# Broadcast weights loaded over all 128 partitions at once: a three-neighbour interpolation kernel

## The chip, the core and the metric

The kernel runs on one core of one Trainium2 chip. The metric is the device time of one execution in microseconds (us). The time before is the median of three runs; one more execution was profiled, and all stretches and waits below are from that one.

## What is computed

For each of 16 batches there are 1024 reference vectors of 64 numbers. Each of 4096 queries names three of them by index and has three weights; the weights are divided by their sum, and the output is the weighted sum of the three vectors.

```python
# features (16, 1024, 64) f32, indices (16, 4096, 3) in 0..1023, weights (16, 4096, 3) f32
weights_norm = weights / (weights.sum(axis=2, keepdims=True) + 1e-8)
for b in range(16):
    for i in range(4096):
        for k in range(3):
            result[b, i] += weights_norm[b, i, k] * features[b, indices[b, i, k]]
```

## The kernel before

The gather is done as a matrix product with one-hot columns. A batch's features lie as 128 rows of eight consecutive vectors; four products of 128 x 128 (two vectors of 64 each, hence the four "planes" j) cover the eight. An index thus splits into a row (7 bits), a plane (2 bits) and a last bit that says which of the two vectors in the 128 output rows is meant.

**Preparation** (`prep`, lines 73 to 135) works on 4096 queries per batch laid out as 128 partitions of 32, for four batches at a time (the first batch alone, then three). VectorE (DVE) turns indices into 16-bit codes, and the weights into two fp16 copies, `wh[0]` and `wh[1]`: a weight stands in the one that its index's last bit names, and the other holds zero there. `put` (line 105) writes codes and both copies to scratch in HBM, `code_d` as [batch, k, query] and `wt_d` as [copy, batch, k, query], in pieces of 32 numbers, 64 bytes.

**Groups.** The main loop runs over groups of 2048 queries, two for each batch; the first batch is cut as 512, 512, 1024, 2048 so that it starts sooner. `load_codes` (151) broadcasts a group's codes from scratch to all 128 partitions of the tile `bcc`. `load_weights` (158) fills the tile `bcw` with two transfers: copy 0 goes to partitions 0 to 63, copy 1 to 64 to 127. In both, a partition's row is three runs of 2048 numbers (4 KB), one for each k. Each tile has three buffers. `load_features` (167) brings a batch's features, `cast_features` (171) makes them fp16 on ScalarE (ACT), in the same order.

**Stages of a chunk of 512 queries.** `stage1` (176): ACT turns codes into bytes `y` with one bit for each plane, set in the partition that the index names. `stage2` (183): DVE takes one bit for each of the four planes, which gives `s`, read as fp8. `main` (192): 12 matmuls of 128 x 512 on TensorE (PE), three k by four planes, into the PSUM tile `acc` (two buffers). `weight` (204): the product with the chunk's part of `bcw` gives `x`; even chunks read PSUM on DVE directly, odd ones through a copy `xc` by ACT. `back` (218): 12 matmuls of 128 x 64 with the matrix `i2` (two identities of 64 over each other) add the two halves of the 128 rows and the three k, and turn the result to queries in rows; it runs two chunks later. Every second chunk ACT copies the result to `og`, and SyncE (SP) starts the output transfer.

**Order.** Every engine works its instructions in the order in which the program gives them (`InOrder`, line 50; so the profile shows line 55 for nearly all, and groups are told apart by tile names). A table `todo` holds a time in chunks for each step: for a group that begins at chunk a, the codes are loaded at a - 12, the weights at a - 7, stage 1 runs from a - 8 on, one piece a chunk, stage 2 from a - 3 on. All transfers are issued by SP, on one queue, and SP waits in order too: an output transfer that waits for its copy holds up the loads behind it.

Of the kernel before, what the change touches and what calls it, by code (L numbers as in the profile page):

```python
# [9 lines left out]
P = 128  # L10
# [3 lines left out]
def kernel(  # L14
# [11 lines left out]
    nc = tc.nc  # L26
    fp32 = mybir.dt.float32
    fp16 = mybir.dt.float16
    fp8 = mybir.dt.float8e4
    i16 = mybir.dt.int16  # L30
# [5 lines left out]
    B, R, D = features.shape  # L36
    _, Q, K = indices.shape
    T = Q // P
    J = 4
    CH = 512  # L40
    GM = 2048
# [16 lines left out]
    pe, ve, ac, sp = (InOrder(e) for e in (nc.tensor, nc.vector, nc.scalar, nc.sync))  # L58

    sb = ctx.enter_context(tc.tile_pool(name="sb", bufs=2))  # L60
    ps = ctx.enter_context(tc.tile_pool(name="ps", bufs=2, space=bass.MemoryType.PSUM))

    i2_np = np.concatenate([np.eye(D), np.eye(D)], 0).astype(np.float16)
    i2_d = nc.inline_tensor(i2_np, name="i2")
    i2 = sb.tile([P, D], fp16, bufs=1, name="i2_sb")
    bias_d = nc.inline_tensor(
        (-8.0 * ((np.arange(P, dtype=np.float32) + 64) % 128 - 64))[:, None].copy(), name="lane")
    bias = sb.tile([P, 1], fp32, bufs=1, name="lane_sb")

    code_d = nc.dram_tensor("code_d", [B, K, Q], i16, kind="Internal")  # L70
    wt_d = nc.dram_tensor("wt_d", [2, B, K, Q], fp16, kind="Internal")

    def prep(b0, n):

        bs = slice(b0, b0 + n)
        NK = n * K

        def tl(dt, w, name):
            return sb.tile([P, PB * w], dt, bufs=1, name=name)[:, 0:n * w]

        idx = tl(i64, T * K, "idx")
        wt = tl(fp32, T * K, "wt")
        wt4 = wt.rearrange("p (b t k) -> p b t k", b=n, k=K)
        idk = tl(i32, K * T, "idk")
        lane = tl(i32, K * T, "lane_i")
        ex = tl(i32, K * T, "ex")
        code = tl(u16, K * T, "code")
        hb = tl(i32, K * T, "hb")
        ws = tl(fp32, T, "ws")
        wi = tl(fp32, T, "wi")  # L90
        wn = tl(fp16, K * T, "wn")
        wh = [tl(fp16, K * T, "wh%d" % h) for h in range(2)]
        v = ve

        def loads():
            sp.dma_start(out=idx.rearrange("p (b t k) -> p b t k", b=n, k=K),
                              in_=indices[bs].rearrange("b (p t) k -> p b t k", t=T))
            sp.dma_start(out=wt4, in_=weights[bs].rearrange("b (p t) k -> p b t k", t=T))

        def weigh(k):  # L100
            v.tensor_tensor(
                out=wn.rearrange("p (b k t) -> p b k t", b=n, k=K)[:, :, k, :],
                in0=wt4[:, :, :, k], in1=wi.rearrange("p (b t) -> p b t", b=n), op=Alu.mult)

        def put(dst, src):
            sp.dma_start(out=dst.rearrange("b k (p t) -> p (b k) t", t=T),
                              in_=src.rearrange("p (x t) -> p x t", t=T))

        return [
            loads,  # L110
            lambda: v.tensor_copy(
                out=idk.rearrange("p (b k t) -> p b k t", b=n, k=K),
                in_=idx.bitcast(i32).rearrange("p (b t k w) -> p b k t w", b=n, k=K, w=2)[:, :, :, :, 0]),
            lambda: v.tensor_scalar(out=lane, in0=idk, scalar1=6, scalar2=127 << 9,
                                    op0=Alu.logical_shift_left, op1=Alu.bitwise_and),
            lambda: v.tensor_scalar(out=ex, in0=idk, scalar1=23, scalar2=3 << 24,
                                    op0=Alu.logical_shift_left, op1=Alu.bitwise_and),
            lambda: v.tensor_scalar(out=ex, in0=ex, scalar1=134 << 23, scalar2=None,
                                    op0=Alu.bitwise_xor),
            lambda: v.scalar_tensor_tensor(out=code, in0=ex.bitcast(fp32), scalar=0.5, in1=lane,  # L120
                                           op0=Alu.mult, op1=Alu.add),
            lambda: put(code_d.ap()[bs], code.bitcast(i16)),
            lambda: v.tensor_reduce(out=ws, in_=wt.rearrange("p (x k) -> p x k", k=K),
                                    axis=mybir.AxisListType.X, op=Alu.add),
            lambda: v.tensor_scalar(out=ws, in0=ws, scalar1=1e-8, scalar2=None, op0=Alu.add),
            lambda: v.reciprocal(out=wi, in_=ws),
            lambda: weigh(0),
            lambda: weigh(1),
            lambda: weigh(2),
            lambda: v.tensor_scalar(out=hb, in0=idk, scalar1=1, scalar2=None, op0=Alu.bitwise_and),  # L130
            lambda: v.tensor_tensor(out=wh[1], in0=wn, in1=hb, op=Alu.mult),
            lambda: v.tensor_tensor(out=wh[0], in0=wn, in1=wh[1], op=Alu.subtract),
            lambda: put(wt_d.ap()[0, bs], wh[0]),
            lambda: put(wt_d.ap()[1, bs], wh[1]),
        ]


    groups = []
    for b in range(B):
        q = 0  # L140
# [8 lines left out]
    bcc, bcw, fsts, f16s, ys, ss = {}, {}, {}, {}, {}, {}  # L149

    def load_codes(g):
        b, q, n, _ = groups[g]
        bcc[g] = sb.tile([P, K * GM], i16, bufs=3, name="bcc")[:, 0:K * n]
        sp.dma_start(
            out=bcc[g].rearrange("p (k q) -> p k q", k=K),
            in_=code_d.ap()[b, :, q:q + n].unsqueeze(0).to_broadcast([P, K, n]))

    def load_weights(g):
        b, q, n, _ = groups[g]
        bcw[g] = sb.tile([P, K * GM], fp16, bufs=3, name="bcw")[:, 0:K * n].rearrange(  # L160
            "p (k q) -> p k q", k=K)
        for h in range(2):
            sp.dma_start(
                out=bcw[g][h * D:(h + 1) * D],
                in_=wt_d.ap()[h, b, :, q:q + n].unsqueeze(0).to_broadcast([D, K, n]))

    def load_features(b):
        fst = fsts[b] = sb.tile([P, J * P], fp32, bufs=2, name="fst")
# [2 lines left out]
    def cast_features(b):  # L171
        fst = fsts[b]
        f16s[b] = sb.tile([P, J, P], fp16, bufs=2, name="f16")
        ac.mul(out=f16s[b].rearrange("p j m -> p (j m)"), in_=fst[:, :], mul=0.5)

    def stage1(g, c):
        if c == 0:
# [65 lines left out]
    for g, (b, q, n, a) in enumerate(groups):  # L243
        m = n // CH
        at(a - 12, 0, load_codes, g)
        at(a - 7, 0, load_weights, g)
        if q == 0:
            at(-11.5 if b == 0 else max(a - 14, -4), 0, load_features, b)
            at(-8.6 if b == 0 else a - 3, 1, cast_features, b)
        for c in range(m):  # L250
            at(a - 2 * m + c if m == 4 else -8.5 + g / 10, 1, stage1, g, c)
        for j in range(J):
            at(a - m + (j * m // J | 1 if m == 4 else 0), 0, stage2, g, j)
    NCH = B * Q // CH
    for b0 in range(PB, B, PB):
        for s, step in enumerate(prep(b0, PB)):
            at((b0 - 4) * (Q // CH) + (s and s + 3), 0, step)
    first, second = prep(0, 1), prep(1, PB - 1)
    at(-20, 0, first[0])
    at(-20, 0, second[0])  # L260
# [71 lines left out]
```

## Time and profile before

| | |
|---|---|
| median of three runs | 529.38 us (524.7 to 532.22) |
| profiled execution, its own time | 525.81 us |
| its span, first to last instruction | 523.7 us |
| mean granted TensorE clock | 0.954 |
| busy: PE, ACT, DVE | 413.8, 320.3, 305.0 us |
| moved by DMA | 125.66 MB, mean 240 GB/s |

In the slices, a span is cut into 40 equal parts, and a digit is the busy share of a part in tenths. A group's row has the engine, the operation, what it writes and reads with shapes and count, then busy time, mean nanoseconds of one, the idle time of the engine before them, and what ended most of that. In the waits: who waited for whom, microseconds in total, how many times, the longest. "x" before a count is the number of instructions. A DMA share of 1.00 means that all 16 DMA engines worked the whole stretch; values just over that come from packets that are counted where they begin.

### The profile page before, as it was taken

Reading aid. Unit: us, or ns where it says so; the run is one execution under the profiler, and the core shown is the slowest. Engines: PE = TensorE matmul, PEld = TensorE weight load, DVE = VectorE, ACT = ScalarE, POOL = GpSimd, SP = SyncE. Lnnn points to the kernel's source line nnn. Section 1 sums busy time; section 2 is a strip of 40 time slices with the busy share of each in tenths; the row PEclk is TensorE's granted clock in tenths of the full one; section 3 lists DMA queues with packets and bytes.
Section 4 is the critical chain, followed back from the end, with each engine's and each line's share of the span. In section 5 each row is a group of like instructions: output and inputs, shape, how many; then the busy total and the mean of one; then the engine's idle time right before and its main releaser. Section 6 shows DMA issues by size and latency. Waiting matters only on the chain.

```text
span 523.7 us, 7372 instructions
## 1 busy us (share of the span) xinstructions
PE 413.8 (79%) x3072; PEld 209.8 (40%) x3072; DVE 305.0 (58%) x335; ACT 320.3 (61%) x274; POOL 0.2 (0%) x4
## 2 busy tenths in 40 slices
PE   0442797968979788978798777987888897998895
PEld 0110353434544444444344333444434443454453
DVE  5142377755556496766466465676646664665672
ACT  1444737765656867756566765567767674667723
POOL 0000000000000000000000000000000000000000
PEclk9986899998998999999999989999989999798998
DMA  3899999899999999899999999889999999999711
GB/s 71 239 175 237 260 258 264 213 262 216 248 283 277 292 283 281 215 235 265 227 284 281 296 273 239 202 208 281 220 260 301 288 281 276 263 266 246 232 41 61
DMA packets 70704, 125.66 MB, mean 240 GB/s; under 512 B 24080, under 2 KB 44048, under 8 KB 70672
## 3 DMA queue, kind: packets, MB, share of 16 engines
q1 hardware_dynamic: 70672, 125.20, 93.4%
q8 instruction: 24, 0.39, 0.3%
q14 instruction: 8, 0.07, 0.0%
HBM read 107.23 MB, written 17.96 MB: 239 GB/s over the span
## 4 chain that ended last, share of the span: by engine, by line
DMA 61%; ACT 12%; PE 10%; SPq 6%; issue 6%; DVE 4%; ACTq 0%
DMA bcc<-code_d 55%; PE acc L55 10%; SPq L55 6%; ACT xc L55 6%; ACT y L55 4%; DMA out_dram<-og 4%; DVE x L55 2%; ACT og L55 2%; DMA fst<-in_features_dram 2%; DVE s L55 1%; ACT f L55 1%; PE pr L55 1%; DMA idx<-in_indices_dram 0%; DMA code_d<-code 0%; ACTq L55 0%
## 5 line engine op out<-in xcount | busy, mean ns | idle before, releaser
L55 PE MATMUL acc<-s,f 128*128 128x512 fp8e4 x1536 | 377.7, 394 | 104.5 <-ACT xc L55 68.2
L55 ACT ACTIVATE y<-bcc,lane_sb 128x1536 uint8<-128x1536 int16 x128 | 198.3, 1577 | 148.5 <-DMA bcc<-code_d 148.5
L55 PEld LDWEIGHTS <-f 128*128 128x128 f16 x1536 | 148.4, 101 | 278.9 <-issue 119.0
L55 DVE TENSOR_TENSOR x<-xc,bcw 128x1536 f16<-128x1536 f16 x64 | 61.3, 958 | 159.1 <-ACT xc L55 158.8
L55 DVE TENSOR_SCALAR s<-y 128x1536 int32<-128x1536 int32 (+2 forms) x136 | 117.1, 905 | 14.6 <-ACT y L55 14.5
L55 DVE TENSOR_TENSOR x<-acc,bcw 128x1536 f16<-128x1536 f32 x64 | 112.2, 1753 | 17.6 <-PE acc L55 14.7
L55 ACT CAST xc<-acc 128x1536 f16<-128x1536 f32 x64 | 91.4, 1428 | 30.8 <-PE acc L55 30.8
L55 PEld LDWEIGHTS <-x 128*128 128x128 f16 x1536 | 71.9, 117 | 31.2 <-DVE x L55 1.8
L55 PE MATMUL pr<-i_sb,x 128*128 128x64 f16 x1536 | 72.2, 198 | 1.7 <-DVE x L55 1.7
L55 ACT COPY og<-pr 128x512 f32<-128x512 f32 x64 | 37.8, 591 | 5.4 <-DMA out_dram<-og 3.9
L55 ACT ACTIVATE f<-fst 128x512 f16<-128x512 f32 x16 | 10.2, 640 | 12.8 <-DMA fst<-in_features_dram 12.8
L55 DVE COPY idk<-idx 128x384 int32<-128x384 int32 (+2 forms) x5 | 2.5, 499 | 21.4 <-DMA idx<-in_indices_dram 21.3
L55 DVE RECIPROCAL wi<-ws 128x128 f32<-128x128 f32 (+2 forms) x5 | 3.9, 789 | 0.1
L55 DVE TENSOR_TENSOR wn<-wt,wi 128x128 f16<-128x128 f32 (+2 forms) x15 | 3.9, 282 | 0.1
L55 ACT ACT_TABLE_LOAD x1 | 1.3, 1283 | 2.8 <-DMA lane_sb<-lane 2.8
L55 DVE SCALAR_TENSOR_TENSOR code<-ex,lane_i 128x384 uint16<-128x384 f32 (+2 forms) x5 | 2.4, 474 | 0.4 <-DMA code_d<-code 0.3
L55 DVE TENSOR_TENSOR wh<-wn,hb 128x384 f16<-128x384 f16 (+2 forms) x5 | 2.4, 475 | 0.1
L55 DVE TENSOR_REDUCE ws<-wt 128x128 f32<-128x384 f32 (+2 forms) x5 | 2.3, 466 | 0.0
L55 DVE TENSOR_SCALAR lane_i<-idk 128x384 int32<-128x384 int32 (+2 forms) x5 | 1.6, 317 | 0.1
L55 DVE TENSOR_SCALAR ex<-ex 128x384 int32<-128x384 int32 (+2 forms) x5 | 1.6, 316 | 0.1
L55 DVE TENSOR_TENSOR wh<-wn,wh 128x384 f16<-128x384 f16 (+2 forms) x5 | 1.6, 314 | 0.1
L55 DVE TENSOR_SCALAR ex<-idk 128x384 int32<-128x384 int32 (+2 forms) x5 | 1.6, 314 | 0.0
(8 smaller groups left out, 3.4 us busy)
## 6 DMA issues: line engine op xcount, KB each, us to landing
bcc<-code_d SPq DMA_DIRECT2D x31, 1536.0 KB, 18.9
bcw<-wt_d SPq DMA_DIRECT2D x62, 768.0 KB, 20.1
out_dram<-og SPq DMA_DIRECT2D x64, 256.0 KB, 14.7
fst<-in_features_dram SPq DMA_DIRECT2D x16, 256.0 KB, 16.1
idx<-in_indices_dram SPq DMA_DIRECT2D x3, 384.0 KB, 21.4
bcc<-code_d SPq DMA_DIRECT2D x2, 384.0 KB, 8.7
bcc<-code_d SPq DMA_DIRECT2D x1, 768.0 KB, 13.1
bcw<-wt_d SPq DMA_DIRECT2D x4, 192.0 KB, 10.0
```

Source lines behind the costliest of these rows:

```text
L55: return tc.keep_in_program_order(getattr(self.engine, op)(*a, **kw))
```

## The change

Three things change together.

1. **Weights.** The two copies go to neighbouring partitions: copy 0 to the even ones, copy 1 to the odd ones, in one transfer over all 128 partitions. Row m of `acc` must then belong to vector m % 2 and number m // 2, so `cast_features` interleaves the two vectors as it writes (a step of two in its output), and `i2` becomes an identity with each row twice. The matmuls, the products and their counts stay.
2. **Scratch.** `code_d` and `wt_d` get a dimension for the half batch ahead of the batch: [half, batch, k, 2048]. A full group's three runs lie one behind the other, so that a partition's row is one run of 6144 numbers (12 KB) for codes and weights. `put` writes each half from its 64 partitions, in two transfers for one.
3. **The smaller groups** of the first batch (512, 512, 1024) load the weights with one transfer for each k, three in place of two.

On SP's queue, in the start: the scratch writes of the first batch's preparation (`wh_109` and `wh_110` are its two copies), then the first code loads and the first features.

```order
-L55 DMA code_d<-code 128x3x32
-L55 DMA wt_d<-wh_109 128x3x32
-L55 DMA wt_d<-wh_110 128x3x32
+L55 DMA code_d<-code 64x3x32 x2
+L55 DMA wt_d<-wh_109 64x3x32 x2
+L55 DMA wt_d<-wh_110 64x3x32 x2
 L55 DMA bcc<-code_d 128x3x512
 L55 DMA fst<-in_features_dram 128x512
```

Three issues became six, ahead of the same first code load. On SP's queue in the middle, at the preparation of the next four batches:

```order
-L55 DMA bcc<-code_d 128x3x2048
-L55 DMA bcw<-wt_d 64x3x2048 x2
-L55 DMA code_d<-code 128x12x32
+L55 DMA bcc<-code_d 128x6144
+L55 DMA bcw<-wt_d 128x1x6144
+L55 DMA code_d<-code 64x12x32 x2
 L55 DMA out_dram<-og 128x2x256
 L55 DMA fst<-in_features_dram 128x512
```

The places stay; the pair of weight loads became one, the write of codes two, and the three runs of a row one. PE, DVE and ACT keep their instructions and their order.

```diff
-    i2_np = np.concatenate([np.eye(D), np.eye(D)], 0).astype(np.float16)
+    i2_np = np.repeat(np.eye(D), 2, axis=0).astype(np.float16)
...
-    code_d = nc.dram_tensor("code_d", [B, K, Q], i16, kind="Internal")
-    wt_d = nc.dram_tensor("wt_d", [2, B, K, Q], fp16, kind="Internal")
+    NG = Q // GM
+    code_d = nc.dram_tensor("code_d", [NG, B, K, GM], i16, kind="Internal")
+    wt_d = nc.dram_tensor("wt_d", [2, NG, B, K, GM], fp16, kind="Internal")
...
         def put(dst, src):
-            sp.dma_start(out=dst.rearrange("b k (p t) -> p (b k) t", t=T),
-                              in_=src.rearrange("p (x t) -> p x t", t=T))
+            h = P // NG
+            for g in range(NG):
+                sp.dma_start(out=dst[g, bs].rearrange("b k (p t) -> p (b k) t", t=T),
+                             in_=src[g * h:(g + 1) * h].rearrange("p (x t) -> p x t", t=T))
...
     def load_codes(g):
         b, q, n, _ = groups[g]
         bcc[g] = sb.tile([P, K * GM], i16, bufs=3, name="bcc")[:, 0:K * n]
-        sp.dma_start(
-            out=bcc[g].rearrange("p (k q) -> p k q", k=K),
-            in_=code_d.ap()[b, :, q:q + n].unsqueeze(0).to_broadcast([P, K, n]))
+        src = code_d.ap()[q // GM, b]
+        if n == GM:
+            sp.dma_start(
+                out=bcc[g],
+                in_=src.rearrange("k q -> (k q)").unsqueeze(0).to_broadcast([P, K * n]))
+        else:
+            sp.dma_start(
+                out=bcc[g].rearrange("p (k q) -> p k q", k=K),
+                in_=src[:, q % GM:q % GM + n].unsqueeze(0).to_broadcast([P, K, n]))
...
     def load_weights(g):
         b, q, n, _ = groups[g]
-        bcw[g] = sb.tile([P, K * GM], fp16, bufs=3, name="bcw")[:, 0:K * n].rearrange(
-            "p (k q) -> p k q", k=K)
-        for h in range(2):
+        w = sb.tile([P, K * GM], fp16, bufs=3, name="bcw")
+        src = wt_d.ap()[:, q // GM, b]
+        if n == GM:
             sp.dma_start(
-                out=bcw[g][h * D:(h + 1) * D],
-                in_=wt_d.ap()[h, b, :, q:q + n].unsqueeze(0).to_broadcast([D, K, n]))
+                out=w[:, :],
+                in_=src.rearrange("h k q -> h (k q)").unsqueeze(0).to_broadcast([D, 2, K * n]))
+            bcw[g] = w.rearrange("p (k q) -> p k q", k=K)
+        else:
+            bcw[g] = w[:, 0:K * n].rearrange("p (k q) -> p k q", k=K)
+            for k in range(K):
+                sp.dma_start(
+                    out=bcw[g][:, k, :],
+                    in_=src[:, k, q % GM:q % GM + n].unsqueeze(0).to_broadcast([D, 2, n]))
...
-        ac.mul(out=f16s[b].rearrange("p j m -> p (j m)"), in_=fst[:, :], mul=0.5)
+        ac.mul(out=f16s[b].rearrange("p j (d h) -> p j h d", h=2),
+               in_=fst.rearrange("p (j h d) -> p j h d", j=J, h=2), mul=0.5)
```

More of the change, by code (lines that the diff above doesn't have):

```diff
@@ L121, in prep @@
                                            op0=Alu.mult, op1=Alu.add),
-            lambda: put(code_d.ap()[bs], code.bitcast(i16)),
+            lambda: put(code_d.ap(), code.bitcast(i16)),
             lambda: v.tensor_reduce(out=ws, in_=wt.rearrange("p (x k) -> p x k", k=K),
@@ L132, in prep @@
             lambda: v.tensor_tensor(out=wh[0], in0=wn, in1=wh[1], op=Alu.subtract),
-            lambda: put(wt_d.ap()[0, bs], wh[0]),
-            lambda: put(wt_d.ap()[1, bs], wh[1]),
+            lambda: put(wt_d.ap()[0], wh[0]),
+            lambda: put(wt_d.ap()[1], wh[1]),
         ]
```

## The prediction

> **What bounds the kernel now.** I read the page's share of DMA time first, then the chain of waits, then the busy time by stage.
>
> ```profile
> DMA  3899999899999999899999999889999999999711
> q1 hardware_dynamic: 70672, 125.20, 93.4%
> DMA 61%; ACT 12%; PE 10%; SPq 6%; issue 6%; DVE 4%; ACTq 0%
> ```
>
> The 16 DMA engines are nine tenths busy or more in nearly every slice. Their packets took 93.4% of 16 engines' span, so 0.934 x 523.7 = 489 us, and DMA is 61% of the chain that ended last. By stage (columns: window, length, busy us and instructions of each engine, granted clock, DMA share, GB/s):
>
> ```profile
> 0.00:30.00 30.00, 7.96 (x24) 3.01 (x24) 12.08 (x41) 9.24 (x8) 0.20 (x4) 1.00 0.68 163
> 30.00:60.00 30.00, 15.64 (x96) 7.28 (x97) 8.91 (x8) 14.74 (x12) 0.00 (x0) 0.77 0.97 228
> 200.00:300.00 100.00, 81.99 (x641) 42.22 (x639) 61.36 (x62) 68.28 (x59) 0.00 (x0) 1.00 1.01 263
> 490.00:524.00 34.00, 27.77 (x239) 14.88 (x237) 19.12 (x17) 14.96 (x15) 0.00 (x0) 0.94 0.22 77
> ```
>
> In the middle the DMA share is 1.01 while PE is 82% busy, and yet only 263 GB/s move. The engines wait for those transfers in this way (waits of the whole span):
>
> ```profile
> ACT y L55 <- DMA bcc<-code_d: 148.5, 33, 10.6
> PE acc L55 <- ACT xc L55: 68.2, 29, 11.6
> PE acc L55 <- DVE s L55: 31.6, 30, 19.8
> ```
>
> ScalarE (ACT) waits for codes; its copies of PSUM stand behind that wait in the same queue, so PE waits for ACT. The DMA queue is the bound, and PE is second.
>
> Does every transfer run at one rate? SP's queue in the start (columns: start, time taken to issue, what, how many):
>
> ```profile
> 34.33 2.48 SPq L55 DMA_DIRECT2D bcw<-wt_d  x2
> 36.91 0.90 SPq L55 DMA_DIRECT2D bcc<-code_d  x1
> 37.85 1.15 SPq L55 DMA_DIRECT2D idx<-in_indices_dram  x1
> 39.05 5.32 SPq L55 DMA_DIRECT2D wt<-in_weights_dram  x1
> ```
>
> A full pair of weight transfers, then one full code transfer, then the next indices and weights. The DMA view of 46 to 52.5 us, then of 53.3 to 54.9 us, then of 146.7 to 149.9 us:
>
> ```profile
> DMA packets 363, 1.38 MB, mean 212 GB/s; under 512 B 27, under 2 KB 27, under 8 KB 363
> q1 hardware_dynamic: 363, 1.38, 103.3%
> ...
> DMA packets 149, 0.61 MB, mean 379 GB/s; under 512 B 1, under 2 KB 1, under 8 KB 149
> q1 hardware_dynamic: 149, 0.61, 98.5%
> ...
> DMA packets 515, 1.34 MB, mean 418 GB/s; under 512 B 24, under 2 KB 243, under 8 KB 515
> ```
>
> All large packets in the first two are of 4 KB, and the engines are full in both, yet the first stretch moves 212 GB/s and the second 379. By the order of the queue the first is the weight pair (1.57 MB at 212 GB/s is 7.4 us, which is what lies ahead of the codes there) and the second the codes. The third stretch, codes mixed with 1 KB output packets, reaches 418. So a transfer to 64 partitions goes at half the rate of one to 128. That is read from the order and the sizes; a packet's row does not name its transfer.
>
> **The change part by part.**
>
> ```profile
> bcc<-code_d SPq DMA_DIRECT2D x31, 1536.0 KB, 18.9
> bcw<-wt_d SPq DMA_DIRECT2D x62, 768.0 KB, 20.1
> bcw<-wt_d SPq DMA_DIRECT2D x4, 192.0 KB, 10.0
> bcw<-wt_d SPq DMA_DIRECT2D x2, 384.0 KB, 6.7
> ```
>
> *Weights in one transfer over 128 partitions.* Per group 2 x 768 KB = 1.57 MB as before. Now 7.4 us at 212 GB/s. No row shows the new transfer; its nearest row is the code load, same destination tile and same bytes: 1.57 MB at 379 to 418 GB/s, 4.15 to 3.76 us. The other bound is no gain, 7.4 us. I take 3.9, by the code load, since what differs from it is only that neighbouring partitions read one of two source rows. Saved: 3.5 us a group, times 32 (31 full groups, and the six smaller transfers, which are one group's bytes) = 112 us; 105 to 117 by the two rates. The engines' busy time goes from 489 to about 377 us.
>
> The Trainium skill has the mechanism: "SBUF — State Buffer", section "Door 1: The DMA port swizzle", says that a DMA's rate is set by how many of 16 ports its partitions reach, that 0 to 63 reach only eight, and that two transfers to the two halves do not add up; it gives asymptotes of 218 and 436 GB/s. The trace agrees, with 212 and 418. A page that speaks against the sum is "DMA: Bandwidth & Descriptors", Specifications: about 358 GB/s of HBM per core. By that the new load would take 4.4 us and save 3.0, 97 us in all; the 418 GB/s of this trace stand above it.
>
> *Contiguous rows of 12 KB.* For codes and weights three runs of 4 KB per partition become one of 12 KB. I take no gain. The bound on the bad side is a rival below; on the good side, fewer and longer pieces cannot do better than the best stretch seen, 418 GB/s, which is inside the range of the first part.
>
> *Scratch writes in two halves.* Six short transfers for three, four times (once a quarter of the batches): twelve more issues. In the start two such issues took 1.02 us:
>
> ```profile
> 7.25 1.02 SPq L55 DMA_DIRECT2D wt_d<-wh  x2
> 19.75 2.80 SPq L55 DMA_DIRECT2D bcw<-wt_d  x4
> 36.91 22.50 DMA bcc<-code_d
> ```
>
> So 0.5 us each, 6 us in all. Three of them stand ahead of the first code load, on the path: +1.5 us. The other nine fall where SP waits for outputs anyway; uncovered they would be 4.5 us. The bytes and their 64-byte pieces stay. The first groups' weights take nine issues instead of six, at 0.7 us each: +2 us of SP, while the engines work off the code loads ahead; uncovered, +2.
>
> *Features written with a stride of two.* Sixteen casts of 640 ns, off PE's path:
>
> ```profile
> L55 ACT ACTIVATE f<-fst 128x512 f16<-128x512 f32 x16 | 10.2, 640 | 12.8 <-DMA fst<-in_features_dram 12.8
> L55 ACT ACTIVATE y<-bcc,lane_sb 128x1536 uint8<-128x1536 int16 x128 | 198.3, 1577 | 148.5 <-DMA bcc<-code_d 148.5
> L55 ACT CAST xc<-acc 128x1536 f16<-128x1536 f32 x64 | 91.4, 1428 | 30.8 <-PE acc L55 30.8
> L55 ACT COPY og<-pr 128x512 f32<-128x512 f32 x64 | 37.8, 591 | 5.4 <-DMA out_dram<-og 3.9
> ```
>
> No row shows the strided form. ACT needs 8 x 1.58 + 4 x 1.43 + 4 x 0.59 + 0.64 = 21.4 us a batch, so even a doubled cast (+0.64) stays under PE's 23.9 below; I take 0, at most 10 us over the run, no gain. The identity has the same shape, and VectorE reads the weights in the same form: 0.
>
> *What is the bound then.* Where nothing is late PE runs at this pace (the chain's last part, then busy time from 451.6 to 472 us):
>
> ```profile
> 508.32 2.59 PE acc L55 x12
> 510.90 0.40 PE pr L55 x12
> 511.30 2.59 PE acc L55 x12
> ...
> 516.92 1.45 ACT xc L55
> ...
> 451.60:472.00 20.40, 20.40 (x160) 10.65 (x158) 13.27 (x12) 13.38 (x13) 0.00 (x0) 1.00 1.04 259
> ```
>
> A chunk is 2.59 + 0.40 = 2.99 us, 23.9 for a batch of eight, and in the second stretch PE is busy all 20.4 us. The other two engines stay below that, 305.0 / 128 = 2.38 and 320.3 / 128 = 2.50 us a chunk:
>
> ```profile
> PE 413.8 (79%) x3072; PEld 209.8 (40%) x3072; DVE 305.0 (58%) x335; ACT 320.3 (61%) x274; POOL 0.2 (0%) x4
> ```
>
> The DMA engines, at 377 us over 16 batches, come to 23.6 us with the start included, so less in the middle. For the whole run: 377 us busy plus the idle parts (0.32 x 30 and 0.78 x 34, 36 us) is 413 us. PE now comes out above it:
>
> - by 60 us PE has 24 + 96 = 120 of 3072 matmuls, five chunks; 123 are left: 123 x 2.99 = 368 us;
> - after the last chunk's matmuls 523.7 - 516.9 = 7 us of copy, product, sum and output remain;
> - 60 + 368 + 7 = 435 us;
> - the start: the codes that landed at 36.91 + 22.50 = 59.4 us had two groups' worth of weights ahead of them (the six small transfers and the pair at 34.33), now 2 x 3.5 = 7 us less; with the 1.5 us above, -5.5;
> - left-over stalls, where the next group's bit planes are just too late (waits within 60 to 520 us):
>
> ```profile
> PE acc L55 <- DVE s L55: 11.9, 29, 0.5
> ```
>
> These are short and hang on VectorE's order, not on the codes alone; I keep 10 us of them, between 0 (the busy stretch has none) and 24 (twice the row).
>
> Sum: 435 - 5.5 + 10 = 439.5 us of span. The profiled execution took 525.81 us for a span of 523.7, so 2.1 us more: **441 us**. That execution is 3.6 us below the median of 529.38, within the runs' 524.7 to 532.22; I add nothing for it.
>
> **The rivals.**
>
> *The new load is faster, but not fully, and the queue stays the bound.* If alternate source rows cost half the gain (5.6 us a load), the engines' time is 489 - 32 x 1.8 = 431, with 36 idle 467 us of span, 469 us. For it: the queue would be near full beside PE even at 377, so outputs and 64-byte writes that bunch up may hold the codes back. Against: a code transfer now waits 19 us to land mostly behind other transfers, and the codes' lead of some four chunks (12 us) covers two loads of 3.9 and two outputs.
>
> *The halves still go at half rate.* If the way in which a transfer with two source rows is dealt to the engines leaves ports shared, nothing is saved: 525.8 + 1.5, 527 us. Against it: every other 128-partition load with full packets runs at the high rate.
>
> *Long pieces are slow, and the kernel becomes slower.* The page has one row with longer packets:
>
> ```profile
> q8 instruction: 24, 0.39, 0.3%
> ```
>
> 0.003 x 16 x 523.7 / 24 = 1.05 us for 16 KB, 15.6 GB/s per engine, where 418 GB/s are 26. At that rate a 12 KB piece takes 0.79 us, eight per engine 6.3 us, and codes and weights of a group 12.6 us instead of 3.9 + 7.4 = 11.3: 32 x 1.3 = +42 us, 568 us. It decides above 5.65 us a load, 0.71 us a piece. Against it: these packets share the engines with the main queue, which is full, so half their time may be waiting.
>
> **How the numbers follow.** Forecast 0.79 (its own range 424 to 455: no left-over stalls and the fuller gain in the start, or 24 us of them); partly faster 0.10; no gain 0.06; slow long pieces 0.05. The range 424 to 485 holds the forecast and the partial case and leaves out the last two, 0.11. A difference from no change can be told at about 2%, 10 us here: faster 0.89 from the first two, same 0.06, slower 0.05.
>
> **What would show it.** Right: bcw issues x31 of 1536 KB; q1's share clearly below 90%; ACT's wait for bcc down from 148.5 us to under 30; PE busy 90% or more with the granted clock at or above 0.954; stretches of many chunks at 2.99 us. The load itself is right if windows of weights alone move about 400 GB/s instead of 212. Wrong: a full DMA row with 200 to 250 GB/s (no gain, or long pieces that are slow), or a DMA row with gaps beside a PE pace well over 2.99 us, which would be a wait that I did not see, in SP's order or between ACT and PE.

## The result and the profile after

The changed kernel takes 427.38 us (median of four runs, 427.06 to 427.65) where the kernel before takes 530.8 (now of four runs, 524.7 to 532.75): a ratio of 0.8082, 95% interval 0.801 to 0.8155. The prediction was 441, within 424 to 485. The profiled execution took 427.65 us with a span of 425.9. (Single executions of experiments 9 and 11 below ran with matmuls one and a half and over four times as long as in the others, and some of the kernel before and of 10 and 11 were a few per cent longer; the medians below count them, the ratios leave them out.)

The page of the changed kernel, the lines that answer to those of before:

```profile
PE 387.8 (91%) x3072; PEld 204.2 (48%) x3072; DVE 307.6 (72%) x335; ACT 323.0 (76%) x274; POOL 0.2 (0%) x4
DMA  2689989989888989999998989989997888986102
q1 hardware_dynamic: 54592, 125.20, 82.3%
PE 88%; DMA 5%; SPq 2%; ACT 2%; DVE 1%; issue 1%; ACTq 0%
...
bcc<-code_d SPq DMA_DIRECT2D x31, 1536.0 KB, 7.4
bcw<-wt_d SPq DMA_DIRECT2D x31, 1536.0 KB, 11.2
```

The same 125.2 MB now take 0.823 x 425.9 = 350.5 us of all 16 engines, where they took 489. The chain that ended last is no longer DMA but PE, 88%. A code load lands in 7.4 us instead of 18.9. By stage (columns as in the prediction):

```profile
0.00:30.00 30.00, 8.15 (x27) 3.16 (x28) 13.83 (x42) 11.93 (x10) 0.20 (x4) 1.00 0.60 169
30.00:60.00 30.00, 19.38 (x130) 9.40 (x128) 15.06 (x16) 18.45 (x15) 0.00 (x0) 0.77 0.97 370
200.00:300.00 100.00, 100.00 (x810) 53.21 (x809) 79.79 (x82) 84.25 (x72) 0.00 (x0) 1.00 0.93 331
400.00:426.00 26.00, 20.23 (x185) 11.15 (x183) 12.31 (x11) 8.29 (x9) 0.00 (x0) 0.96 0.15 52
...
40.00:60.00 20.00, 16.82 (x107) 8.04 (x107) 13.23 (x14) 16.14 (x13) 0.00 (x0) 0.79 1.03 414
```

PE is busy all of the 100 us in the middle. The stretch from 40 to 60 us, in which codes and weights follow one another, moves 414 GB/s with full engines. The prediction asked for a stretch of weights alone. Here is one: SP issued a code load at 74.81 us, which landed at 82.2, and the weight load behind it at 75.38, which landed at 87.3. All packets of the stretch are over 8 KB; a row of codes or weights is 12 KB.

```profile
82.30:84.70 2.40, 2.40 (x23) 1.33 (x22) 2.40 (x3) 1.96 (x3) 0.00 (x0) 1.00 1.00 423
```

The weights move at 423 GB/s with full engines, where the old pair moved at 212. The waits of the whole span:

```profile
PE acc L55 <- DVE s L55: 20.0, 1, 20.0
PE acc L55 <- ACT xc L55: 10.6, 1, 10.6
ACT y L55 <- DMA bcc<-code_d: 10.2, 3, 7.9
```

Each of PE's two long waits happened once, in the start, where ACT's three waits for codes lie too. Nothing is left of the repeated wait.

PE's busy time fell too, from 413.8 to 387.8 us for the same 3072 matmuls, which is 26 of the 97.8 us by which the span is shorter. An example from the kernel before (its PE timeline, then its table):

```profile
445.89 5.28 PE L55 MATMUL acc<-s,f 128*128 128x512 fp8e4 x12 [4.15 <-ACT xc L55]
```

```profile
445.90:451.00 5.10, 5.10 (x13) 1.80 (x13) 4.33 (x4) 3.36 (x3) 0.00 (x0) 0.50 1.04 264
```

Behind a wait of 4.15 us the granted clock was 0.50, and the chunk's twelve matmuls took 5.28 us where they take 2.75 in a stretch without gaps. So a long wait cost PE twice.

### The profile page after: what moved, and what is told of

Same layout as the page of the kernel before. It is cut to its first block, busy times and chain, and to the rows that moved or that the text cites. A ratio compares the mean times of both kernels' runs of the same rounds, so it can differ in the third digit from the quotient of the medians.

```text
span 425.9 us, 7346 instructions
## 1 busy us (share of the span) xinstructions
PE 387.8 (91%) x3072; PEld 204.2 (48%) x3072; DVE 307.6 (72%) x335; ACT 323.0 (76%) x274; POOL 0.2 (0%) x4
## 3 DMA queue, kind: packets, MB, share of 16 engines
q1 hardware_dynamic: 54592, 125.20, 82.3%
## 4 chain that ended last, share of the span: by engine, by line
PE 88%; DMA 5%; SPq 2%; ACT 2%; DVE 1%; issue 1%; ACTq 0%
PE acc L55 77%; PE pr L55 12%; DMA bcc<-code_d 4%; SPq L55 2%; DMA idx<-in_indices_dram 1%; ACT y L55 1%; ACT xc L55 1%; DVE s L55 0%; DVE idk L55 0%; ACT og L55 0%; DVE ex L55 0%; DVE x L55 0%; DVE lane_i L55 0%; ACTq L55 0%
## 5 line engine op out<-in xcount | busy, mean ns | idle before, releaser
L55 PE MATMUL acc<-s,f 128*128 128x512 fp8e4 x1536 | 357.1, 383 | 32.5 <-DVE s L55 20.0
L55 PEld LDWEIGHTS <-f 128*128 128x128 f16 x1536 | 143.4, 99 | 187.4 <-ACT f L55 18.2
L55 ACT ACTIVATE y<-bcc,lane_sb 128x1536 uint8<-128x1536 int16 x128 | 194.7, 1575 | 10.2 <-DMA bcc<-code_d 10.2
L55 ACT ACTIVATE f<-fst 128x512 f16<-128x512 f32 x16 | 12.6, 790 | 13.0 <-DMA fst<-in_features_dram 13.0
## 6 DMA issues: line engine op xcount, KB each, us to landing
bcw<-wt_d SPq DMA_DIRECT2D x31, 1536.0 KB, 11.2
```

The lines of the kernel that those rows point to most:

```text
L55: return tc.keep_in_program_order(getattr(self.engine, op)(*a, **kw))
```

## The experiments

The theory: a transfer's rate hangs on which partitions it reaches; one half of them gives half the rate, and with full rate the DMA queue falls below PE. Rivals: the 12 KB rows or the new scratch did it; or one transfer in place of two did it.

| | kernel | median us | against before, same chip |
|---|---|---|---|
| 1 | even and odd partitions, old scratch, 4 KB runs | 429.51 | 0.8099 (0.8051 to 0.8146) |
| 2 | new scratch, 12 KB rows, weights in halves | 502.35 | 0.9465 (0.9395 to 0.9535) |
| 3 | even and odd partitions, two transfers | 431.95 | 0.8134 (0.8084 to 0.8185) |
| 4 | one transfer, copies in the two halves | 1233.63 | one execution |
| 5 | as 2, padded scratch, 4 KB runs | 514.87 | 0.9676 (0.9585 to 0.9766) |
| 6 | changed, codes in halves | 487.45 | one execution |
| 7 | changed, fourth plane left out | 366.58 | one execution |
| 8 | changed, second batch's stage 1 later | 427.06 | 0.8012 (0.7974 to 0.805) |
| 9 | changed, start reordered | 428.77 | 0.8076 (0.8008 to 0.8144) |
| 10 | before, padded scratch | 530.77 | 0.9916 (0.9848 to 0.9984) |
| 11 | before, scratch writes in halves | 543.93 | none |
| 12 | as 9 | 427.56 | 0.8045 (0.7985 to 0.8105) |

**1. The partitions alone.** Beside the new `cast_features` and `i2`:

```diff
-        for h in range(2):
-            sp.dma_start(
-                out=bcw[g][h * D:(h + 1) * D],
-                in_=wt_d.ap()[h, b, :, q:q + n].unsqueeze(0).to_broadcast([D, K, n]))
+        for k in range(K):
+            sp.dma_start(
+                out=bcw[g][:, k, :],
+                in_=wt_d.ap()[:, b, k, q:q + n].unsqueeze(0).to_broadcast([D, 2, n]))
```

> The kernel before with the weights alone changed: even and odd partitions over all 128, one transfer for each k, in runs of 4 KB from the old scratch; one write to scratch in place of two. If the reach over 128 partitions is the cause (my theory), 427 us, within 5, and PE at 2.99 us a chunk: the 4 KB pieces cost 3 x 159 = 477 ns a row where the changed kernel has 460. If the contiguous 12 KB rows are the cause, it stays near the kernel before, 515 to 530. If one transfer in place of two is the cause, it is no faster than before, since here there are three.

Measured 429.5. This part alone gives all but 2 us of the whole gain, with three transfers where there were two. From 60 to 400 us, this kernel and then the changed one:

```profile
60.00:400.00 340.00, 340.00 (x2736) 180.50 (x2734) 266.85 (x269) 286.26 (x243) 0.00 (x0) 1.00 0.98 322
```

```profile
60.00:400.00 340.00, 340.00 (x2736) 180.53 (x2734) 266.41 (x268) 284.37 (x242) 0.00 (x0) 1.00 0.89 318
```

PE runs without a gap in both. But with the old scratch and its 4 KB runs the DMA share is 0.98, with the new one and its 12 KB rows 0.89: scratch and rows together bring room that PE does not need.

**2. The scratch and the rows alone.** The weights go to the halves again, for a full group so:

```diff
-            sp.dma_start(
-                out=w[:, :],
-                in_=src.rearrange("h k q -> h (k q)").unsqueeze(0).to_broadcast([D, 2, K * n]))
+            for h in range(2):
+                sp.dma_start(
+                    out=w[h * D:(h + 1) * D, :],
+                    in_=src[h].rearrange("k q -> (k q)").unsqueeze(0).to_broadcast([D, K * n]))
```

> The changed kernel with the new scratch and 12 KB rows, but the weights in two transfers, copy 0 to partitions 0 to 63 and copy 1 to 64 to 127, features and identity as before. By my theory the weights move at about 212 GB/s again, the DMA engines are full, and the time is 510 to 530 us. If contiguous rows or the scratch layout were the cause, 427 to 440.

Measured 502.4, below the 510 that was expected: the rows and the scratch are worth 5% where the queue is the bound. It stays the bound, as the stretch from 60 to 460 us shows, first of this kernel, then of the one before:

```profile
60.00:460.00 400.00, 346.93 (x2655) 178.16 (x2652) 258.57 (x264) 272.22 (x233) 0.00 (x0) 0.98 1.00 273
```

```profile
60.00:460.00 400.00, 335.36 (x2507) 170.64 (x2507) 246.95 (x254) 261.24 (x224) 0.00 (x0) 0.97 1.01 259
```

Both have a full DMA row, 273 and 259 GB/s. A stretch of this kernel's weights alone, behind codes that landed at 227.4 us:

```profile
227.60:230.80 3.20, 3.20 (x27) 1.69 (x25) 0.52 (x2) 3.20 (x4) 0.00 (x0) 1.00 0.99 211
```

In rows of 12 KB, too, the halves move at 211 GB/s with full engines.

**3. Two transfers of 64 partitions, but every second one.** In the changed kernel, for a full group:

```diff
-            sp.dma_start(
-                out=w[:, :],
-                in_=src.rearrange("h k q -> h (k q)").unsqueeze(0).to_broadcast([D, 2, K * n]))
+            for h in range(2):
+                sp.dma_start(
+                    out=w[h::2, :],
+                    in_=src[h].rearrange("k q -> (k q)").unsqueeze(0).to_broadcast([D, K * n]))
```

> The changed kernel with its weight load cut in two transfers of 64 partitions, the even ones and then the odd ones. If the half rate comes from which partitions a transfer reaches (only 0 to 63, or 64 to 127), each of these still reaches over the whole range and goes at full rate: 427 to 432 us. If it comes from a transfer having 64 rows, or from two transfers instead of one, 510 to 530.

Measured 432.0. A stretch of weights alone, behind codes that landed at 84.1 us:

```profile
84.30:86.00 1.70, 1.70 (x10) 0.80 (x8) 1.70 (x3) 1.55 (x2) 0.00 (x0) 1.00 1.06 448
```

448 GB/s at a share of 1.06 is 423 at a share of one. The pair has the size and the number of the one in experiment 2 and runs at twice its rate, so neither 64 rows nor two transfers was the cause; which partitions they are was. The time is 4.6 us over the changed kernel's; the landing of the loads and PE's waits in this kernel:

```profile
bcw<-wt_d SPq DMA_DIRECT2D x62, 768.0 KB, 9.7
...
PE acc L55 <- ACT xc L55: 14.6, 4, 11.1
```

PE waits four times for ACT instead of once, 14.6 us in place of 10.6. That is most of the 4.6 us; why the three short waits come is not shown.

**4. One transfer that is not interleaved.** As 2, but copy 0 to the lower and copy 1 to the upper half in one transfer:

```diff
-            for h in range(2):
-                sp.dma_start(
-                    out=w[h * D:(h + 1) * D, :],
-                    in_=src[h].rearrange("k q -> (k q)").unsqueeze(0).to_broadcast([D, K * n]))
+            sp.dma_start(
+                out=w[:, :],
+                in_=src.rearrange("h k q -> h (k q)").unsqueeze(1).to_broadcast([2, D, K * n]))
```

> One transfer over all 128 partitions, but copy 0 to the lower half and copy 1 to the upper: the source's outer dimension has two entries, each repeated 64 times. Features and identity as before. If only the reach of a transfer counts, 427 us. The Trainium skill, DMA: Bandwidth & Descriptors, section Why a DMA increments its semaphore by 16 and not by 1, says that the outermost dimension sets how many engines work, here two: then a load moves at about two sixteenths of 418 GB/s, 52, takes 30 us, and the time is 1000 us or more.

Measured 1233.6, more than twice the time before. A stretch of this kernel's table, its queue's row, and its waits:

```profile
330.00:340.00 10.00, 0.09 (x1) 0.09 (x1) 1.76 (x1) 1.27 (x2) 0.00 (x0) 0.50 0.13 53
```

```profile
q1 hardware_dynamic: 54110, 125.20, 31.1%
```

```profile
DVE x L55 <- DMA bcw<-wt_d: 604.6, 29, 24.4
```

A share of 0.13 is two engines of 16 (0.125), and 53 GB/s is 26 for each, the full rate of an engine (418 / 16). This agrees with the rule of the Trainium skill, DMA: Bandwidth & Descriptors, section Why a DMA increments its semaphore by 16 and not by 1, that the expectation goes by. So the reach over 128 partitions is not enough by itself: for one transfer, the two copies had to be interleaved so that the source's outer dimension is the 64 repeats and not the two copies.

**5. Long rows or their place?** As 2, with the scratch's last dimension padded; codes and weights are then loaded in three runs for every group:

```diff
-    code_d = nc.dram_tensor("code_d", [NG, B, K, GM], i16, kind="Internal")
-    wt_d = nc.dram_tensor("wt_d", [2, NG, B, K, GM], fp16, kind="Internal")
+    code_d = nc.dram_tensor("code_d", [NG, B, K, GM + 128], i16, kind="Internal")
+    wt_d = nc.dram_tensor("wt_d", [2, NG, B, K, GM + 128], fp16, kind="Internal")
```

> Experiment 2 again (weights in halves, 502 us), with 256 bytes of padding behind each k in the scratch, so that rows are again three pieces of 4 KB, at almost the same places in HBM. If the 28 us that experiment 2 gained over the kernel before come from the longer pieces, this loses them: 525 to 535 us. If they come from where the scratch lies, or from the writes in two halves, it stays at 498 to 506.

Measured 514.9, between the two: by the ratios, of the 28 us some 11 go with the length of the pieces and some 17 stay (each ratio is known to about 1%, 5 us).

**10 and 11. Where those 17 come from.** Experiment 10 is the kernel before with 128 numbers of padding behind each k, experiment 11 the kernel before with this:

```diff
-            sp.dma_start(out=dst.rearrange("b k (p t) -> p (b k) t", t=T),
-                              in_=src.rearrange("p (x t) -> p x t", t=T))
+            h = P // 2
+            for g in range(2):
+                sp.dma_start(out=dst[:, :, g * GM:(g + 1) * GM].rearrange("b k (p t) -> p (b k) t", t=T),
+                             in_=src[g * h:(g + 1) * h].rearrange("p (x t) -> p x t", t=T))
```

> The kernel before with 256 bytes of padding behind each k of the scratch, so that its runs of 4 KB no longer lie exactly 8 KB apart; nothing else. It asks where experiment 5's 3% came from. If from the distance between runs in HBM, 512 to 520 us; if from the writes in two halves, 527 to 534 as before.

> The kernel before with each scratch write cut in two transfers of 64 partitions, as the changed kernel has it; scratch and loads unchanged. If the writes in halves gave experiment 5 its 3%, 512 to 520 us; by the prediction's count of issues they cost up to 6 us, 530 to 537; if the distance of the runs in HBM gave it, 527 to 534.

Padding alone gave 530.8, 0.9916 of before: under 1%, not 3. The four executions with writes in halves lie between 527.5 and 2311 us, too far apart for a ratio; the shortest is not below the shortest of the kernel before on that chip (525.7), so no gain of 3% shows. Where the 17 us come from stays open.

**6. The other load in halves.** In the changed kernel, for a full group:

```diff
-            sp.dma_start(
-                out=bcc[g],
-                in_=src.rearrange("k q -> (k q)").unsqueeze(0).to_broadcast([P, K * n]))
+            for h in range(2):
+                sp.dma_start(
+                    out=bcc[g][h * D:(h + 1) * D],
+                    in_=src.rearrange("k q -> (k q)").unsqueeze(0).to_broadcast([D, K * n]))
```

> The changed kernel with the code load, not the weight load, cut in two transfers to partitions 0 to 63 and 64 to 127. If the half rate belongs to the reach of a transfer and to nothing about the weights, the code load now takes twice as long, the DMA engines are full again, and the time is as in experiment 2, 495 to 510 us. If it was peculiar to the weights, 427 to 435.

Measured 487.5, 8 us under the range; the direction and most of the size are as expected. The DMA engines are full again:

```profile
60.00:460.00 400.00, 360.41 (x2791) 186.51 (x2789) 272.07 (x276) 288.81 (x247) 0.00 (x0) 0.99 1.00 282
```

Halving the reach of a load that was fast costs 60 us in this one execution; it was nothing peculiar to the weights. Why the time is 15 us below that of experiment 2 is not shown.

**7. Is PE the bound now?**

```diff
-            for j in range(J):
+            for j in range(J - 1):
...
-                                 start=(j == 0), stop=(j == J - 1))
+                                 start=(j == 0), stop=(j == J - 2))
```

> The changed kernel without the matmuls of the fourth plane (9 of 12 first-stage matmuls a chunk; queries whose code lies in that plane get zero). PE needs 9 x 0.216 + 0.40 = 2.34 us a chunk instead of 2.99. If PE was the bound with the DMA engines close behind (a share of 0.92 at 2.99, so 2.75 us a chunk), it becomes 48.7 + 124 x 2.75 + 10 = 400 us, within 8. If DMA has more room than its share says, ACT is next at 2.52 us a chunk: 371. If PE was not the bound, 425 to 428.

Measured 366.6: PE was the bound, since taking a quarter of its first-stage work away took 61 us. But the next bound was mis-sized. From 60 to 300 us:

```profile
60.00:300.00 240.00, 229.67 (x2012) 124.98 (x2011) 220.03 (x229) 234.95 (x203) 0.00 (x0) 1.00 1.02 387
```

With 21 matmuls a chunk, 2012 in 240 us are 2.50 us a chunk, the pace that the expectation gave for ACT (2.52), and ACT is busy 235 of 240 us. The DMA engines, full too, move 387 GB/s, where they moved 331 at a share of 0.93: scaled to a share of one that would have been 356, which is how the 400 us came about. Here a share below one did not scale with the load.

**8, 9 and 12. The start.** The changed kernel begins its fifth chunk only at 48.7 us, so a version was tried that begins sooner. In experiment 8 `stage1` for the group at chunk 8 stands at 3 + c // 2 in the table. In 9 this holds for the groups at 8, 12 and 16, and the next preparation comes later:

```diff
-            at(a - 2 * m + c if m == 4 else -8.5 + g / 10, 1, stage1, g, c)
+            at((a - 5 + c // 2 if 8 <= a <= 16 else a - 2 * m + c) if m == 4 else -8.5 + g / 10,
+               1, stage1, g, c)
...
-            at((b0 - 4) * (Q // CH) + (s and s + 3), 0, step)
+            at((b0 - 4) * (Q // CH) + (8 + (s and 3 + s // 2) if b0 == PB else s and s + 3), 0, step)
```

> The changed kernel with the second batch's first stage 1 pieces three chunks later in the order (chunks 3, 3, 4, 4 in place of 0, 1, 2, 3), so that ACT's first PSUM copies no longer stand behind codes that land at 40 us. PE's wait of 10.6 us before the fourth chunk goes. If that wait is what the start loses, the time falls by 6 to 11 us, to 416 to 422. If weights or codes that are late for the next chunks take its place, 425 to 428.

Measured 427.1, no gain. The fourth chunk began at 33.9 us instead of 43.2, as meant, and then (PE's and ACT's timelines of experiment 8):

```profile
45.28 0.56 PE L55 MATMUL pr<-i_sb,x 128*128 128x64 f16 x12
52.55 4.09 PE L55 MATMUL acc<-s,f 128*128 128x512 fp8e4 x12 [6.71 <-ACT xc L55]
```

```profile
49.60 1.57 ACT L55 ACTIVATE y<-bcc,lane_sb 128x1536 uint8<-128x1536 int16 x1 [3.13 <-DMA bcc<-code_d]
```

The next batch's codes are the next thing ACT waits for, ahead of the copy that PE needs.

> The changed kernel with the start's order mended in two ways after experiment 8: stage 1 of the groups that begin at chunks 8, 12 and 16 comes three chunks later in ACT's order, and the preparation of the second four batches, its loads of indices and weights included, starts eight chunks later, two steps a chunk. Experiment 8 got the sixth chunk's matmuls to end near 45 us and then waited to 52.5 us for ACT, which stood behind codes landing at 49.5, and DVE behind indices. If the order of work behind late transfers is what the start loses, chunks run on from 45 us and the time falls by 5 to 9 us, to 418 to 422. If the DMA queue itself is what the start is bound by, another load is late instead and the time is 425 to 428.

> Experiment 9 once more, since its profiled execution ran with matmuls of two thirds of the usual pace, while its other executions (427.1 to 429.3 us) did not. The question is what is late in the start when chunks run at 2.99 us. If the DMA queue bounds the start, the profile shows PE or DVE waiting for a transfer again between 40 and 60 us (weights of the group at chunk 4, or codes of the group at chunk 12), the ninth chunk begins at 60 us as in the changed kernel (60.7), and the time is 425 to 429 us. If instead the matmuls themselves go slower than 2.99 us a chunk later on, the ninth chunk begins near 54 us and the pace shows it. If experiment 9 was only disturbed, 418 to 422.

Measured 428.8 and 427.6. The profile of 12 fits neither theory: PE is ahead when the ninth chunk begins, and gives it back later (PE's timeline, then ACT's):

```profile
55.59 2.75 PE L55 MATMUL acc<-s,f 128*128 128x512 fp8e4 x12
...
77.98 2.75 PE L55 MATMUL acc<-s,f 128*128 128x512 fp8e4 x12 [3.13 <-ACT xc L55]
```

```profile
69.16 7.44 ACT L55 ACTIVATE y<-bcc,lane_sb 128x1536 uint8<-128x1536 int16 x5
```

The ninth chunk begins at 55.6 us, 5.1 us sooner than in the changed kernel (60.7). But where the later places in the table meet the usual ones, five pieces of stage 1 stand in a row on ACT, 7.4 us, and PE waits for the copy behind them. From 60 to 100 us PE is busy 36.1 us of 40. No version beat the changed kernel by more than 0.3 us.

## Why the prediction was right, and where its sizes were off

**The mechanism** is as forecast: the weights ran at half rate for the partitions that they reached (1, 2, 3 and 6), the queue fell below PE, and PE took over at 2.99 us a chunk (7). The signs named beforehand came: bcw x31, q1 at 82.3%, ACT's wait for codes 10.2 us, PE busy 91%, granted clock 0.982, weights alone at 423 GB/s.

**The sum** was 13.6 us of span too high, 439.5 against 425.9. Term by term:

- *The start*, -5.5: by 60 us PE had 27 + 130 = 157 matmuls, 37 more than before; 37 / 24 x 2.99 = 4.6 us. The size is nearly right, in part by luck. The code load that the term names, the second full one, landed at 48.2 us instead of 59.4, 11.2 us sooner; what let PE go on sooner was the load ahead of it, which landed at 40.2 us instead of 45.5, and the fourth chunk began at 43.2 instead of 48.5.
- *Left-over stalls*, +10: none. From 60 us until its last chunk PE has no wait. The waits for bit planes that this term kept were not VectorE's order by itself: where the queue is the bound they are there (35, 35 and 26 times in experiments 2, 5 and 6), and with the same order and a faster load only the one of the start is left (the changed kernel, 1 and 3). They came with the late codes. This is the largest miss.
- *The end*: the 7 us behind the last chunk were added to a count of matmuls that held the last 36 `pr` matmuls already, 36 / 24 x 2.99 = 4.5 us counted twice.

439.5 + 0.9 - 10 - 4.5 = 425.9. The small terms were sound: the first code load was issued at 10.74 us instead of 8.90, 1.84 us later where 1.5 was priced, and the strided cast takes 790 ns instead of 640, 2.4 us of ACT in all and off PE's path.

**Contiguous rows**, taken at no gain: right for the time (experiment 1 is 2 us slower without them), wrong for the queue. Together with the new scratch they cut the DMA share from 0.98 to 0.89 at the same pace, and gave 5% where the queue was the bound (2); the length of the pieces is some 11 of those 28 us (5), the rest is not explained. The 377 us foretold for the engines were 350.5; experiment 1, with the old scratch and 4 KB runs, has 0.900 x 429.0 = 386, so the difference lies in scratch and rows.

**The rivals.** That long pieces are slow, drawn from a row of 16 KB packets, is out: 423 GB/s in 12 KB pieces. That ports stay shared is out for the interleaved form, but experiment 4 shows that the danger lay next to it: another order of the same two dimensions would have cost 700 us. The partly faster case did not come; experiment 1 is how near it was, with a share of 0.98.

## What to carry to other kernels

Where a queue is full, split its bytes by transfer and compare GB/s at equal share: here packets of one size at 212 and 379 GB/s named the transfer to mend. A load to partitions 0 to 63 and one to 64 to 127 went at half rate each, and every second partition at full rate. In one transfer look at the outermost dimension of the source: with 64 entries all engines worked, with two only two. When a gain moves the bound to another engine, price the new bound by its own gap-free stretch, and do not carry over waits that the old bound had caused.

## What the runs showed of the hardware

- A source whose outer dimension has two entries ran on two DMA engines: a share of 0.13 at 53 GB/s.
- 64 partitions in steps of two ran at full rate (448 GB/s at a share of 1.06), 64 neighbouring ones at half (211 at 0.99).
- The new scratch, with rows of 12 KB instead of three runs of 4 KB, lowered the DMA share by 0.09 for the same work at the same pace.
- The DMA engines' share did not scale with the bytes: 331 GB/s at 0.93, and 387 at 1.02 with PE's work cut.
- Behind a wait of 4.15 us PE ran at a granted clock of 0.50, and a chunk's first-stage matmuls took 5.28 us instead of 2.75.
